# A sum of w_o weights computed two quarter products earlier, and two row turnings one step earlier

## The chip, the cores and the metric

The kernel runs on one core of one Trainium2 chip. A core has five engines with queues of their own: TensorE (PE) multiplies matrices, VectorE (DVE) and ScalarE (ACT) do elementwise work and read the results of PE out of PSUM, GpSimd (POOL) does a little elementwise work and issues some transfers, and SyncE (SP) issues most transfers. Each engine takes its instructions strictly in the order in which they stand in its queue, and engines wait for each other by semaphores.

The metric is the device time of one execution in microseconds, as a median over runs. The kernel before takes 1021.9 us.

## What is computed

One layer of a decoder trunk: a normed input is projected, three mixers (attention, pooling, a state-space scan) are gated and merged, the merged rows are multiplied by `w_o` and added to the input, and the result is normed again and goes through a gated feed-forward block. Everything is float32, with 512 rows (`SEQ`) of 1024 features (`D_MODEL`). The part around the change is this:

```python
merged = gates[:, :, 0] * y_a + gates[:, :, 1] * y_b + gates[:, :, 2] * y_c
x = x + merged @ w_o[i]
x = x + conv_ffn(rmsnorm(x, ln2_g[i]), ffn_w_up[i], ffn_conv_w[i], ffn_conv_b[i], ffn_w_down[i])

def rmsnorm(x, g):
    y = xf * lax.rsqrt(jnp.mean(xf * xf, axis=-1, keepdims=True) + NORM_EPS)
    return (y * g.astype(jnp.float32)).astype(x.dtype)
```

So the rows of `merged @ w_o` are added to `x`, each row is normed over its 1024 features, and the normed rows are the input of the product with `ffn_w_up`.

## The kernel before

Every float32 operand of a matmul is held as two parts of a shorter type: a high part, and a low part that is the operand minus its high part. A product is three passes, high by high, high by low and low by high (`mm3`, L230). For a tile of weights `cast` (L185) writes the high part with two copies on ACT (L195) and `lows` (L210) writes the low part with one subtraction on DVE (L217, tile `wl`).

The program is a list of jobs, and a job is one product with one tile of weights. The loop at L1834 runs over them. Ahead of job n it prepares others (`prepare`, L1841): the low parts of job n+1 on DVE, the casts of job n+2 on ACT, and the load of job n+3. Where `once` is set the casts go out at once; where it isn't they are spread over the next steps (`flush`, L138). Where a job has a `form`, its weights are first computed by it; with `lazy` that is put off to the first spread cast. A job with `late` runs its own preparation inside its body. `step` (L155) advances side work: a generator put into `running` goes on by one `yield` at each step.

PE, ACT, DVE and POOL keep the order in which this program emits their instructions. SP's order is chosen by a scheduler at build time. A pool of tiles hands a buffer out again once its last reader is done: the pool of raw weights (`wraw`, L94) has two buffers and the pool of `W` tiles (`ypool`, L99) has three, so a load waits on SP for the reader that frees its buffer, and what stands behind it on SP waits too.

`merged @ w_o` is `wo_group` (L1265). It is cut into 2 x 2 blocks and done in seven quarter products instead of eight, on sums of blocks. Each multiplies two blocks of 128 rows by 512 features into 512 columns, in 2 x 12 matmuls. In order of execution they are `two`, `five`, `three`, `one`, `six`, `seven`, `four`. The first three share a pair of PSUM banks B, the last four the pair A, on which they pile up: `one` starts the pair, `six`, `seven` and `four` add to it. After each half product DVE reads its bank and adds it to a tile of the new rows `X1` (L1351). The next product may not write a bank before that read is over.

The sums of weights are computed on DVE by `total` (L1376). `W[2]` is `W[0] + W[1]` (L1291). `W[1]` is overwritten by `W[2]` minus the quarter of `one` (L1389). The weights of `four`, the last ones, are a loaded quarter plus `W[2]` (L1387); this sum is lazy, so it is emitted while `six` runs, right after the first read of `six`.

The norm goes on between the products. `first` (L1293) is called behind `one` and `seven`: squares of the first half of a row block on ACT (L439, tile `junk`), a small scale on DVE (L463, L1297), and a multiplication by the gain on POOL (L464, tile `xg`). `then` (L1300) is called behind `six` and `four`, with the second half: squares (L439), a square root on ACT (L473, ahead of the first of which ACT loads a table of functions), reciprocal and scale on DVE (L478 to L483), and the two normed halves, one on DVE (L487) and one on ACT (L488), both tiles named `u`. `norm_turn` (L449) then turns the block: eight transposes on PE into two PSUM banks of the tag `sm` (L453, tile `uT`), two copies on ACT (L456, `uh`), two subtractions on DVE (L457, `ul`). There are four row blocks, tb 0 to 3. For tb 0 and 1 the turning sits in a generator put into `running` with `rest(3)`; for tb 2 and 3 it is called by hand from `opening` (L1522), the first product with `ffn_w_up` (L1533, tile `pu`), which needs the turned rows of tb 0 and 1 and then the low parts of its own weights.

A side item of the same stage is `ff_cols` (L1403): three small loads on SP (L512), two transposes on PE (L518) into two more `sm` banks and two copies on DVE (L519). The tag `sm` has four banks (L101).

## Time and profile before

| | |
|---|---|
| median of 3 runs | 1021.9 us (1021.67 to 1021.9) |
| the profiled execution's own time | 1021.8 us |
| its span, first to last instruction | 1020.0 us |
| PE busy | 1006.3 us (99%) |
| DVE busy | 719.4 us (71%) |
| ACT busy | 518.3 us (51%) |
| POOL busy | 143.8 us (14%) |

All rows come from one profiled execution, and times in them are microseconds from the start of its span. A row of the timeline gives the start, the duration, the engine, the line of the kernel, the operation, the tiles (written <- read), the shapes and how many instructions are merged in it; in square brackets stands how long the engine had been idle before, and what ended that. Instructions of one engine overlap a little, so what an instruction costs its engine is read from its start to the start of the next one. A row of waits gives who waited for whom, the sum in microseconds, how often, and the longest. A row of windows gives the busy time of each engine in a stretch and, under PEclk, the granted clock of TensorE as a share of its full speed.

### The profile page before, as it was taken

What the parts mean: (1) busy time and instruction counts of PE and PEld (TensorE: products, weight loads), DVE (VectorE), ACT (ScalarE), POOL (GpSimd) and SP (SyncE); (2) the same over time, 40 slices, a digit from 0 to 9 for tenths busy, and PEclk for the clock granted to TensorE, in tenths of its full rate; (3) what the DMA queues carried; (4) which work ended last, traced back from release to release, by engine and by line L of the source; (5) the groups of instructions that cost most, each with busy time, mean ns of one, the idle gap of its engine ahead of it and who ended that gap; (6) DMA issues with size and microseconds to landing.
All of it is one profiled execution on the core that took longest, in us unless ns stands there. A gap on an engine that the chain in (4) does not pass through costs nothing.

```text
span 1020.0 us, 13623 instructions
## 1 busy us (share of the span) xinstructions
PE 1006.3 (99%) x5378; PEld 857.5 (84%) x5378; DVE 719.4 (71%) x910; ACT 518.3 (51%) x877; POOL 143.8 (14%) x128
## 2 busy tenths in 40 slices
PE   9999999999999999999999999899999999999997
PEld 8998878999988888888888887698888888888885
DVE  6564768677757647667888787758778768685756
ACT  5433546564435476879566335554444444433434
POOL 1791000010000000000063501102111100111002
PEclk9999999999999999999999999999999999999999
DMA  8548312155254343552256346332332322321332
GB/s 271 168 104 206 101 66 77 56 155 162 95 182 108 90 126 103 145 143 84 83 161 160 124 145 163 129 125 83 105 103 83 105 101 84 124 83 42 124 103 83
DMA packets 114623, 121.26 MB, mean 119 GB/s; under 512 B 6499, under 2 KB 96166, under 8 KB 114559
## 3 DMA queue, kind: packets, MB, share of 16 engines
q1 hardware_dynamic: 111087, 114.81, 36.7%
q0 software_dynamic: 2880, 4.72, 2.8%
q8 instruction: 42, 0.69, 0.3%
q10 hardware_dynamic: 592, 0.86, 0.2%
q14 instruction: 22, 0.18, 0.1%
HBM read 116.58 MB, written 3.00 MB: 117 GB/s over the span
## 4 chain that ended last, share of the span: by engine, by line
PE 95%; DVE 3%; ACT 1%; DMA 1%; issue 0%; ACTq 0%; DVEq 0%
PE pa L238 36%; PE pu L238 22%; PE pb L238 9%; PE pd L238 7%; PE pqk L238 6%; PE pq L238 3%; PE pa L1750 2%; PE ps L786 1%; PE ppw L238 1%; PE po L834 1%; DVE wl L217 1%; PE pt L820 1%; PE py L1119 1%; PE pu L1533 1%; DMA xin<-in_x_dram 1%; ACT junk L439 1%
## 5 line engine op out<-in xcount | busy, mean ns | idle before, releaser
L217 DVE TENSOR_TENSOR wl<-raw,wh 128x2048 fp32r<-128x2048 f32 (+3 forms) x87 | 203.5, 2339 | 47.8 <-ACT wh L195 34.1
L195 ACT CAST wh<-raw 128x1024 fp32r<-128x1024 f32 (+4 forms) x171 | 171.7, 1020 | 68.4 <-DVE raw L361 17.8
L1428 DVE SCALAR_TENSOR_TENSOR hc<-pu,fcol,hc 128x510 f32<-128x510 f32 x88 | 65.8, 748 | 56.4 <-ACT hc L1425 54.8
L238 PE MATMUL pa<-uh,wh 128*128 128x512 f32 (+1 forms) x368 | 88.8, 381 | 0.0
L238 PE MATMUL pa<-ul,wh 128*128 128x512 f32 (+1 forms) x368 | 86.8, 375 | 0.0
L238 PE MATMUL pa<-uh,wl 128*128 128x512 f32 (+1 forms) x368 | 86.7, 375 | 0.0
L238 PE MATMUL pu<-uh,wh 128*128 128x512 f32 (+1 forms) x352 | 83.6, 379 | 0.0
L238 PE MATMUL pu<-ul,wh 128*128 128x512 f32 (+1 forms) x352 | 83.5, 379 | 0.0
L238 PE MATMUL pu<-uh,wl 128*128 128x512 f32 (+1 forms) x352 | 83.5, 379 | 0.0
L238 PEld LDWEIGHTS pa<-ul,wh 128*128 128x128 f32 x368 | 66.7, 188 | 12.6
L238 PEld LDWEIGHTS pa<-uh,wl 128*128 128x128 f32 x368 | 66.7, 188 | 12.5
L238 PEld LDWEIGHTS pa<-uh,wh 128*128 128x128 f32 x368 | 65.4, 189 | 11.8
L238 PEld LDWEIGHTS pu<-ul,wh 128*128 128x128 f32 x352 | 64.2, 188 | 12.5
L238 PEld LDWEIGHTS pu<-uh,wl 128*128 128x128 f32 x352 | 64.2, 188 | 12.4
L238 PEld LDWEIGHTS pu<-uh,wh 128*128 128x128 f32 x352 | 64.1, 188 | 12.4
L1425 ACT ACTIVATE hc<-pu,fcol,fcol 128x512 f32<-128x512 f32 x40 | 31.2, 779 | 79.1 <-PE pu L238 79.1
L1433 POOL TENSOR_TENSOR hc<-hc 128x512 f32<-128x512 f32 x22 | 30.8, 1399 | 286.4 <-DVE hc L1428 252.1
L217 DVE TENSOR_TENSOR wl<-w,wh 128x2048 fp32r<-128x2048 f32 (+1 forms) x22 | 47.3, 2149 | 10.2 <-issue 4.6
L808 ACT ACTIVATE sb<-sb,nmls 128x128 f32<-128x128 f32 (+1 forms) x72 | 30.0, 418 | 31.5 <-DVE nmls L805 20.8
L195 ACT CAST wh<-w 128x1024 fp32r<-128x1024 f32 (+1 forms) x44 | 41.0, 971 | 4.8 <-PE pb L238 2.4
L1102 POOL TENSOR_TENSOR st<-st,dts 128x512 f32<-128x512 f32 x4 | 4.2, 1049 | 226.1 <-ACT st L1110 164.0
L1430 ACT ACTIVATE hc<-hc 128x512 f32<-128x512 f32 x22 | 13.9, 632 | 39.9 <-DVE hc L1428 39.8
(424 smaller groups left out, 1948.4 us busy)
## 6 DMA issues: line engine op xcount, KB each, us to landing
raw<-in_w_in_dram SPq DMA_DIRECT2D x24, 1024.0 KB, 5.5
raw<-in_ffn_w_up_dram SPq DMA_DIRECT2D x22, 1024.0 KB, 5.3
raw<-in_ffn_w_down_dram SPq DMA_DIRECT2D x8, 1024.0 KB
raw<-in_w_in_dram SPq DMA_DIRECT2D x14, 512.0 KB, 5.8
raw<-in_w_in_dram SPq DMA_DIRECT2D x8, 768.0 KB
raw<-in_w_b_dram SPq DMA_DIRECT2D x4, 1024.0 KB
al<-ad SPq DMA_DIRECT2D x16, 256.0 KB, 6.5
raw<-in_w_c_dram SPq DMA_DIRECT2D x4, 1024.0 KB, 5.4
```

The source lines that it names most:

```text
L195: (other.tensor_copy if other and i else act.copy)(job.high[:, :, o], job.raw[:, :, o])
L217: (eng or dve).tensor_tensor(l[:, :, o], job.raw[:, :, o], h[:, :, o].bitcast(F32), OP.subtract)
L238: pe.matmul(ps, l, r, start=first and n == 0, stop=last and n == total - 1, skip_group_check=onto)
L439: act.activation(junk, src, AF.Square, accum_out=ss)
L786: pe.matmul(pss[i][:, o:o + w * P], q[r, n * P:(n + 1) * P], k[r, kb * P:(kb + w) * P], start=True, stop=True)
L808: act.activation(sb[:, off:off + w * P], sb[:, off:off + w * P], AF.Exp, bias=nm[:, n, h:h + 1], accum_out=ls[:, n, h:h + 1])
L820: pe.transpose(pt[:, o:o + P], sb[:, o:o + P], eye)
L1425: act.activation(t, ps, AF.Identity, bias=ff["c1"][:, ff["b"] + m:ff["b"] + m + 1], scale=fw(2, m))
L1428: dve.scalar_tensor_tensor(t[:, sh:], ps[:, :S - sh], fw(k, m), t[:, sh:], OP.mult, OP.add)
L1430: act.activation(t, t, AF.Silu)
L1433: pool.tensor_tensor(a, a, t, OP.mult)
L1750: pe.matmul(first[2 * n + j][:, lo:hi], a[:, k, j * P:(j + 1) * P], b[:, k, lo:hi], start=a is wh and b is uh and k == 0, stop=a is wl and ...
```

## The change

```diff
             if tb < 2:
-                running.append(rest(3))
+                running.append(rest(2))
             elif tb == 2:
...
+        def one_read(tb):
+            first(tb, 1)
+            if tb == 0:
+                total(four.raw, four.raw, W[2])
+
         two = job("A12", quarter(1, 0), None, B, (0, 0), apart=True, fresh=True)
         five = job(1, None, lambda: W[0], B, (1, 1), apart=True, fresh=True)
         three = job(4, None, lambda: W[1], B, (0, 1), more=True)
-        one = job("A11", quarter(0, 0), None, A, (0, 0), behind=lambda tb, h: first(tb, 1))
+        one = job("A11", quarter(0, 0), None, A, (0, 0), behind=lambda tb, h: one_read(tb))
         six = job(2, None, lambda: W[2], A, (0, 1), more=True, op=OP.subtract, behind=then)
         seven = job(3, None, lambda: W[1], A, (1, 1), more=True, op=OP.subtract,
                     behind=lambda tb, h: first(tb, 0))
-        four = job("A22", quarter(1, 0), lambda: total(four.raw, four.raw, W[2]), A, (1, 0), more=True,
+        four = job("A22", quarter(1, 0), None, A, (1, 0), more=True,
                    behind=then)
         one.then = lambda: total(W[1], W[2], one.raw, OP.subtract)
-        six.once, four.lazy = False, True
+        def early():
+            four.load = None
+            fetch(four)
+            four.load = lambda: None
+
+        six.load = early
         four.late, inner = True, four.body
```

The sum for `four` is now emitted behind the first read of `one`, instead of behind the first read of `six`. The load of its quarter is emitted with the preparation of `five`, where `six` used to load nothing, instead of with that of `one`. `four` has no `form` and isn't lazy any more, and `six.once` stays true, so the two casts of `four` go out together at the head of `six`, instead of one in each half of it. The turnings of tb 0 and tb 1 run one step earlier.

In the order of instructions as built this moves the following, and nothing else. On DVE the sum (L1377) stands ahead of the second read of `one`, and the subtractions of tb 0's turning (L457) ahead of the second read of `seven`, those of tb 1's ahead of the first read of `four`. On ACT the two casts stand ahead of the squares of the first half of `six`, and the copies of the turnings (L456) move up likewise. On PE the transposes of tb 0 stand between the two halves of `seven`, right behind those of `ff_cols`, and the transposes of tb 1 between `seven` and `four`; before, they stood between `seven` and `four` and between the halves of `four`. In both kernels tb 1's transposes take the two `sm` banks of `ff_cols` and wait for the copies L519; in the changed one `four` stands behind them in PE's queue. On SP the load of the quarter of `four` keeps its place; one load of `ffn_w_down` (L1481 before, L1491 after) moves ahead of the three loads of `ff_cols`.

## The prediction

> **What bounds the kernel now.** I read the chain of waits first, then the waits of the stage that the change touches (600 to 690 us), then its timelines of PE and DVE.

> ```profile
> PE 95%; DVE 3%; ACT 1%; DMA 1%; issue 0%; ACTq 0%; DVEq 0%
> ```

> PE sets the end, so an edit counts by the PE time that it opens or closes.

> ```profile
> PE pb L238 <- DVE x L1351: 3.0, 2, 1.5
> ```

> Two of PE's waits in this stage are for reads of its banks, and the timeline shows a third of the same length, for the turned rows: 4.5 us together, which is all that can be won.

> ```profile
> 640.64 1.07 PE L238 MATMUL pb<-wh,sah 128*128 128x512 f32 x4
> ...
> 643.37 1.07 PE L238 MATMUL pb<-wh,sbh 128*128 128x512 f32 x4
> ...
> 646.09 0.27 PE L518 MATMUL fcol0p<-eye,fcol0r 128*128 128x128 f32 x1
> ...
> 648.04 1.21 PE L238 MATMUL pb<-wh,sbh 128*128 128x512 f32 x4 [1.49 <-DVE x L1351]
> ...
> 650.94 1.03 PE L453 MATMUL uT<-eye,u 128*128 128x128 f32 x8
> 653.45 1.17 PE L238 MATMUL pb<-wh,mgh 128*128 128x512 f32 x4 [1.47 <-DVE x L1351]
> ...
> 656.30 1.03 PE L453 MATMUL uT<-eye,u 128*128 128x128 f32 x8
> 657.09 1.17 PE L238 MATMUL pb<-wh,mgh 128*128 128x512 f32 x4
> ...
> 661.56 2.18 PE L1533 MATMUL pu<-uh,wh 128*128 128x256 f32 x16 [1.49 <-ACT uh L456]
> ...
> 665.50 1.03 PE L453 MATMUL uT<-eye,u 128*128 128x128 f32 x8
> 666.63 2.18 PE L1533 MATMUL pu<-uh,wl 128*128 128x256 f32 x16
> ```

> The halves of `seven` start at 643.37 and 648.04, those of `four` at 653.45 and 657.09, the opening of the next product at 661.56. Each half ends in a read on DVE, and the reads stand in DVE's queue among everything else:

> ```profile
> 637.15 0.15 DVE L1297 TENSOR_SCALAR vo<-v 128x1 f32<-128x1 f32 x1
> 638.12 0.69 DVE L1351 TENSOR_TENSOR x<-x,pb 128x512 f32<-128x512 f32 x1 [0.82 <-PE pb L238]
> ...
> 639.86 2.47 DVE L217 TENSOR_TENSOR wl<-w,wh 128x2048 fp32r<-128x2048 f32 x1
> 642.25 0.68 DVE L1351 TENSOR_TENSOR x<-x,pb 128x512 f32<-128x512 f32 x1
> ...
> 643.80 2.29 DVE L1377 TENSOR_TENSOR raw<-raw,w 128x2048 f32<-128x2048 f32 x1
> 646.00 0.16 DVE L481 RECIPROCAL r<-sq 128x1 f32<-128x1 f32 x1
> ...
> 646.64 0.75 DVE L487 SCALAR_TENSOR_TENSOR u<-x,rt,grow 128x512 f32<-128x512 f32 x1
> 647.31 0.68 DVE L1351 TENSOR_TENSOR x<-x,pb 128x512 f32<-128x512 f32 x1
> ...
> 652.63 0.68 DVE L1351 TENSOR_TENSOR x<-x,pb 128x512 f32<-128x512 f32 x1
> ...
> 654.36 0.28 DVE L519 COPY fcol<-fcol0p 128x128 f32<-128x128 f32 x1
> ...
> 654.67 0.68 DVE L1351 TENSOR_TENSOR x<-x,pb 128x512 f32<-128x512 f32 x1
> ...
> 656.61 1.29 DVE L457 TENSOR_TENSOR ul<-uT,uh 128x512 fp32r<-128x512 f32 x2
> 657.81 0.68 DVE L1351 TENSOR_TENSOR x<-x,pb 128x512 f32<-128x512 f32 x1
> ...
> 661.54 1.29 DVE L457 TENSOR_TENSOR ul<-uT,uh 128x512 fp32r<-128x512 f32 x2 [0.53 <-ACT uh L456]
> 662.74 0.68 DVE L1351 TENSOR_TENSOR x<-x,pb 128x512 f32<-128x512 f32 x1
> ...
> 664.29 2.28 DVE L217 TENSOR_TENSOR wl<-raw,wh 128x2048 fp32r<-128x2048 f32 x1
> ```

> The reads pace PE: at 643.80 the moved sum stands between two reads, 2.20 us from its start to that of the next. The last row matters most: PE's start at 666.63 is the end of that subtraction plus 0.06. So the stage is a chain through DVE and ACT, and the question is when the instruction of 664.29 starts.

> **The sum, step by step along DVE.** The sum can start right behind the scale, at 637.15 + 0.07 = 637.22; PE makes DVE wait there 0.82 today. Its cost is 2.20 at least. It may be 2.39: the subtraction at 639.86 took 2.47 where the same-sized sum took 2.29, and POOL was busy during its start:

> ```profile
> 636.26 1.29 POOL L464 TENSOR_TENSOR xg<-x,grow 128x512 f32<-128x512 f32 x1 [6.98 <-DVE x L1351]
> 638.89 1.29 POOL L464 TENSOR_TENSOR xg<-x,grow 128x512 f32<-128x512 f32 x1 [1.34 <-DVE x L1351]
> ```

> The sum would start 0.33 before POOL's earlier row ends, as the subtraction did before the later one, so I lean to 2.39 and keep both. The second read of `one` then starts at 639.42 to 639.61 instead of 638.12: 1.30 to 1.49 late. It ends by 640.3, and the half of `six` that needs its bank starts at 640.64: no stall, by 0.3. The first read of `six` follows 4.13 behind, as before (638.12 to 642.25): 643.55 to 643.74.

> There the old gain is due: without the sum, the way to the next read should shrink by 2.20. It doesn't, since the reciprocal needs the square root, and that a table:

> ```profile
> 643.70 1.28 ACT L473 ACT_TABLE_LOAD   x1
> 645.00 0.30 ACT L473 ACTIVATE sq<-ss,v 128x1 f32<-128x1 f32 x1
> 646.17 1.04 ACT L195 CAST wh<-raw 128x1024 fp32r<-128x1024 f32 x1 [0.88 <-DVE r L481]
> ```

> The load starts 1.45 behind the read and the root is done 3.05 behind it. With 0.03 for the semaphore the reciprocal can start 3.08 behind, where today it starts 3.75 behind (642.25 to 646.00). Of 2.20 only 0.67 comes back; the sum had covered the load. The next read follows the reciprocal by 1.31: 647.94 to 648.13, 0.63 to 0.82 late. The two casts of `four`, 1.04 each (the last row is one of them), now stand ahead of this on ACT, between the squares of the second read of `one` (done near 641) and the first read of `six` at 643.55: they fit. [...]

> Low parts of `four` and the first read of `seven`: 5.32 on, unchanged, 653.26 to 653.45. The copy of `ff_cols` 1.73 behind that: 654.99 to 655.18. Then the subtractions of tb 0's turning, 1.20 for the pair (656.61 to 657.81), ahead of the second read of `seven`: 2.04 + 1.20 behind the first, 656.50 to 656.69. On to the first read of `four` the queue holds tb 1's pair where it held tb 0's: 3.14 as before, 659.64 to 659.83. From there the pair of 661.54 and the 0.53 waited ahead of it are gone: 4.93 - 1.73 = 3.20, or 3.11 with the overlap of neighbours, so the last read starts at 662.75 to 663.03 instead of 662.74. Everything behind it is as before. **Net: 0.0 to 0.3 us, taken as 0.2.** Saved are the two waits of 0.82 and 0.53, and they are paid for by the table load.

> **The same on PE**, to see that it isn't later. The first half of `seven` waits for the read of `six` (0.73 from its start): 644.3 to 644.5, 0.9 to 1.1 late. It ends 2.72 later, at 647.0 to 647.2, the small transposes take until 647.7, and tb 0's `u` is written 1.39 behind the reciprocal, 648.0 to 648.2. Its eight transposes take 0.79 (656.30 to 657.09). The second half of `seven`, 2.90 long, starts at 648.8 to 649.0 and ends at 651.7 to 651.9. Now tb 1's transposes stand ahead of `four` and wait for the copy of 654.99: 655.3 to 655.5. **PE stands still for about 3.6 us in one piece**, where it stood 1.47. Then 0.79, 2.85 and 2.73: `four` begins at 656.1 to 656.3, and the opening at 661.7 to 661.9 (before, 661.56). The first half of `four` ends 0.5 before DVE reads it. The opening's first two passes take 3.94 and the transposes 0.79, so PE is ready at 666.4 to 666.6 for a subtraction that is done at 666.64 to 666.93. PE has 0.2 to 0.3 to spare.

> **Loads.**

> ```profile
> 611.60 0.38 SPq L182 DMA_DIRECT2D raw<-in_w_o_dram  x1
> ...
> 632.01 0.54 SPq L512 DMA_DIRECT2D fcol0r<-in_ffn_conv_w_dram  x1
> ...
> 642.39 4.11 SPq L1481 DMA_DIRECT2D w<-in_ffn_w_down_dram  x2
> ```

> The quarter of `four` is issued at 611.60, once its buffer is free, and that stays: the moved load is worth nothing either way. The first of the two `ffn_w_down` loads goes out when the sum frees `W[2]`, at 639.5 instead of 642.39, and the three loads of `ff_cols` now wait behind it, from 632.0 to about 640. PE needs them at 647; a delay up to about 652 falls into the standstill of 3.6.

> **Rivals.** *PE's clock falls in the long standstill* (slower).

> ```profile
> 645.00:650.00 5.00, 3.51 (x16) 2.59 (x15) 3.83 (x11) 3.91 (x8) 0.00 (x0) 1.00 0.86 316
> ...
> 1013.40:1017.00 3.60, 0.00 (x0) 0.00 (x0) 2.57 (x7) 1.74 (x4) 0.00 (x0) 1.00 0.38 146
> 1017.00:1020.00 3.00, 0.00 (x0) 0.00 (x0) 0.00 (x0) 0.00 (x0) 0.00 (x0) 0.50 0.45 175
> ```

> Behind the last matmul the clock stays at 1.00 for 3.6 us and is then 0.50; a stop of 1.5, which lies in the first of these stretches, left it at 1.00. It decides from a stop of about 3.6 on, which is what I work out. If half speed lasts as long as it took to come, 3.6 us, PE loses 1.8, less the 0.2 to spare: 1021.8 + 0.2 + 1.6 = 1023.6. If it lasts over the transposes and both halves of `four`, 6.4 us are lost: 1028.2. Against it: a stop just short of the limit costs nothing. [...]

> *The table load starts earlier or is hidden* (faster): then the reciprocal waits its 1.28 less, 1022.0 - 1.3 = 1020.7. Against it: the load stands behind the squares in ACT's order. *All three stops close*: 1021.8 - 4.45 = 1017.4. Against it: DVE's chain above; it needs PE to bound the stage.

> *The loads of `ff_cols` are late* (slower). They were issued at 632.01 and used at 646.09, so they take 14.1 at most. From 640.5 that is 654.6; with the small transposes, tb 0's and the second half of `seven` (0.5 + 0.79 + 2.90) tb 1's would start at 658.8, 3.3 late, less the 0.5 by which `four` is early for its read: 1022.0 + 2.8 = 1024.8. For it: a whole 1 MB load now stands ahead of them. Against it: they need be no faster than 11.

> **How the numbers follow.** The profiled execution took 1021.8, 0.1 under the median of 1021.9. Forecast: 1021.8 + 0.2 = 1022.0, its own range 1021.5 to 1022.4. Chances: forecast 0.58; clock 0.18, of which 0.10 near 1023.6 and 0.08 beyond; table hidden 0.07; stops closed 0.06; late loads 0.06; something unseen 0.05, mostly slower. Two runs of this kernel can be told apart from about 0.2%, 2.0 us: forecast, near clock and hidden table lie within, 0.75; slower 0.08 + 0.06 + 0.03 = 0.17; faster 0.06 + 0.02 = 0.08. The range goes from the hidden table to the first clock case and the late loads, 1020.5 to 1024.8.

> **What would show it.** Right: the sum at 637.2, the read behind it 1.3 to 1.5 late, the reciprocal 3.1 behind the first read of `six`, one stop of PE of 3 to 4 us ahead of tb 1's transposes released by L519, none ahead of the opening, and the start of 666.63 within 0.4 of that. Wrong: a granted clock under 1.00 near 655, a stop of PE at L518 released by a transfer, or two reads of `seven` closer than 3 us.

## The result, and the profile after

| | before | after |
|---|---|---|
| median | 1022.04 us (1021.64 to 1022.77, 22 runs) | 1023.58 us (1021.7 to 1027.55, 22 runs) |
| the profiled execution's own time | 1021.8 us | 1024.06 us |
| its span | 1020.0 us | 1022.3 us |
| its mean granted clock | 0.999 | 0.997 |

After over before is 1.0017, 95% interval 1.001 to 1.0024. That is under the 0.2% that the prediction called no change, and inside its range, but it isn't the forecast of 1022.0: it is the time of the first rival, 1023.6.

Of the 2.26 us between the two profiled executions, 0.69 are there before the changed part begins: DVE's small scale ahead of the moved sum stands at 637.15 in the profile before and at 637.84 after. Nearly all of it (0.66) comes from the start of the run, where DVE's first scaling of `xin` stands at 19.59 and 20.25. That start differs between the profiled executions here (19.51 in `banks_free` to 21.24 in `fill`). So all distances below are counted from that scale, L1297, which I call the mark. DVE's timeline after (start, duration, engine, line, operation, tiles, shapes):

```profile
637.84 0.15 DVE L1297 TENSOR_SCALAR vo<-v 128x1 f32<-128x1 f32 x1
637.91 2.47 DVE L1377 TENSOR_TENSOR raw<-raw,w 128x2048 f32<-128x2048 f32 x1
640.31 0.68 DVE L1351 TENSOR_TENSOR x<-x,pb 128x512 f32<-128x512 f32 x1
...
644.43 0.68 DVE L1351 TENSOR_TENSOR x<-x,pb 128x512 f32<-128x512 f32 x1
...
647.50 0.16 DVE L481 RECIPROCAL r<-sq 128x1 f32<-128x1 f32 x1 [1.45 <-ACT sq L473]
...
648.82 0.68 DVE L1351 TENSOR_TENSOR x<-x,pb 128x512 f32<-128x512 f32 x1
...
654.14 0.68 DVE L1351 TENSOR_TENSOR x<-x,pb 128x512 f32<-128x512 f32 x1
...
655.87 0.28 DVE L519 COPY fcol<-fcol0p 128x128 f32<-128x128 f32 x1
...
657.37 0.68 DVE L1351 TENSOR_TENSOR x<-x,pb 128x512 f32<-128x512 f32 x1
...
661.74 0.69 DVE L1351 TENSOR_TENSOR x<-x,pb 128x512 f32<-128x512 f32 x1 [1.14 <-PE pb L238]
...
666.41 2.29 DVE L217 TENSOR_TENSOR wl<-raw,wh 128x2048 fp32r<-128x2048 f32 x1
```

Down to 657.37 every row stands within 0.01 of the upper end of what the prediction worked out for it (less 0.69: 637.22, 639.62, 643.74, 648.13, 653.45, 655.18, 656.68). The wait of 1.45 in front of the reciprocal, 3.07 behind the read of 644.43, is the table load laid bare. ACT's timeline after:

```profile
645.88 1.28 ACT L473 ACT_TABLE_LOAD   x1
647.18 0.29 ACT L473 ACTIVATE sq<-ss,v 128x1 f32<-128x1 f32 x1
```

Then the row of 661.74, the first read of `four`, waits for PE, which was meant to be half a microsecond early. PE's timeline and windows say why (in a window's row, PEclk stands behind the five engines' busy times, ahead of the DMA share):

```profile
651.76 1.07 PE L238 MATMUL pb<-wl,sbh 128*128 128x512 f32 x4
656.29 1.06 PE L453 MATMUL uT<-eye,u 128*128 128x128 f32 x8 [3.46 <-DVE fcol L519]
657.12 1.82 PE L238 MATMUL pb<-wh,mgh 128*128 128x512 f32 x4
658.73 1.91 PE L238 MATMUL pb<-wh,mgl 128*128 128x512 f32 x4
660.44 1.26 PE L238 MATMUL pb<-wl,mgh 128*128 128x512 f32 x4
661.54 1.09 PE L238 MATMUL pb<-wh,mgh 128*128 128x512 f32 x4
...
664.28 2.08 PE L1543 MATMUL pu<-uh,wh 128*128 128x256 f32 x16
666.20 2.08 PE L1543 MATMUL pu<-ul,wh 128*128 128x256 f32 x16
668.12 1.04 PE L453 MATMUL uT<-eye,u 128*128 128x128 f32 x8
668.91 2.15 PE L1543 MATMUL pu<-uh,wl 128*128 128x256 f32 x16
```

```profile
655.00:657.40 2.40, 1.10 (x9) 1.13 (x10) 1.76 (x7) 1.53 (x4) 1.16 (x1) 1.00 0.79 244
657.40:660.80 3.40, 3.40 (x9) 2.67 (x8) 2.25 (x6) 1.69 (x4) 1.28 (x1) 0.50 0.40 136
660.80:665.00 4.20, 4.20 (x23) 3.53 (x21) 2.19 (x7) 1.74 (x4) 0.00 (x0) 1.00 0.00 0
```

The one long stop is there, 3.46 us, released by L519. Behind it four matmuls of `four` take 1.6 to 1.7 us from start to start instead of 0.91, for 3.4 us, in which the granted clock is 0.50. The clock doesn't fall in the stop, but 1.1 us behind its end. The third pass of the opening starts 668.91 - 637.84 = 31.07 behind the mark. Before it was 666.63 - 637.15 = 29.48: 1.59 more. Nothing waits in front of it now: PE goes from the transposes of 668.12 straight on, so PE has become the bound.

### The profile page after: what moved, and what is told of

It is laid out like the page before. It is cut to its first block, busy times and chain, and to the rows that moved or that the text cites. A ratio compares the mean times of both kernels' runs of the same rounds, so it can differ in the third digit from the quotient of the medians.

```text
span 1022.3 us, 13624 instructions
## 1 busy us (share of the span) xinstructions
PE 1007.1 (99%) x5378; PEld 858.1 (84%) x5378; DVE 718.6 (70%) x910; ACT 518.7 (51%) x877; POOL 143.7 (14%) x128
## 4 chain that ended last, share of the span: by engine, by line
PE 96%; DVE 2%; DMA 1%; ACT 1%; issue 0%; ACTq 0%; DVEq 0%
PE pa L238 36%; PE pu L238 22%; PE pb L238 10%; PE pd L238 7%; PE pqk L238 6%; PE pq L238 3%; PE pa L1760 2%; PE ps L786 1%; PE pu L1543 1%; PE ppw L238 1%; PE po L834 1%; PE pt L820 1%; PE py L1119 1%; DVE wl L217 1%; DMA xin<-in_x_dram 1%; PE pyo L1126 1%
## 5 line engine op out<-in xcount | busy, mean ns | idle before, releaser
L217 DVE TENSOR_TENSOR wl<-raw,wh 128x2048 fp32r<-128x2048 f32 (+3 forms) x87 | 202.7, 2330 | 47.6 <-ACT wh L195 33.9
L195 ACT CAST wh<-raw 128x1024 fp32r<-128x1024 f32 (+4 forms) x171 | 171.5, 1020 | 63.4 <-DVE raw L361 17.8
L238 PE MATMUL pa<-uh,wh 128*128 128x512 f32 (+1 forms) x368 | 88.8, 381 | 0.0
L238 PE MATMUL pa<-ul,wh 128*128 128x512 f32 (+1 forms) x368 | 86.8, 375 | 0.0
L238 PE MATMUL pa<-uh,wl 128*128 128x512 f32 (+1 forms) x368 | 86.8, 375 | 0.0
L238 PE MATMUL pu<-uh,wh 128*128 128x512 f32 (+1 forms) x352 | 83.5, 379 | 0.0
L238 PE MATMUL pu<-ul,wh 128*128 128x512 f32 (+1 forms) x352 | 83.5, 379 | 0.0
L238 PE MATMUL pu<-uh,wl 128*128 128x512 f32 (+1 forms) x352 | 83.5, 379 | 0.0
L238 PEld LDWEIGHTS pa<-ul,wh 128*128 128x128 f32 x368 | 66.7, 188 | 12.6
L238 PEld LDWEIGHTS pa<-uh,wl 128*128 128x128 f32 x368 | 66.7, 188 | 12.5
L238 PEld LDWEIGHTS pa<-uh,wh 128*128 128x128 f32 x368 | 65.4, 189 | 11.8
L238 PEld LDWEIGHTS pu<-uh,wl 128*128 128x128 f32 x352 | 64.2, 188 | 12.5
L238 PEld LDWEIGHTS pu<-ul,wh 128*128 128x128 f32 x352 | 64.2, 188 | 12.5
L238 PEld LDWEIGHTS pu<-uh,wh 128*128 128x128 f32 x352 | 64.1, 188 | 12.4
L217 DVE TENSOR_TENSOR wl<-w,wh 128x2048 fp32r<-128x2048 f32 (+1 forms) x22 | 47.3, 2151 | 10.2 <-issue 4.6
L195 ACT CAST wh<-w 128x1024 fp32r<-128x1024 f32 (+1 forms) x44 | 41.0, 971 | 4.8 <-PE pb L238 2.4
```

Source lines behind the costliest of these rows:

```text
L195: (other.tensor_copy if other and i else act.copy)(job.high[:, :, o], job.raw[:, :, o])
L217: (eng or dve).tensor_tensor(l[:, :, o], job.raw[:, :, o], h[:, :, o].bitcast(F32), OP.subtract)
L238: pe.matmul(ps, l, r, start=first and n == 0, stop=last and n == total - 1, skip_group_check=onto)
```

## The experiments

Each kernel ran together with the kernel before on one chip. Two measures are given beside the time: the distance from the mark to the third pass in the profiled execution, and how many of the runs had a mean granted clock of 0.997 or less. In the profiles a clock that falls only behind the last matmul gives 0.998 (`fill`) to 0.999 (before); one stretch of 3.41 us at half speed more gives 0.996 (`turn_only`) to 0.997 (after). Of the kernel before 13 runs of 100 beside these were so too, at 1024.3 to 1025.3, none of them with a profile.

**PE's stop filled.** Twelve matmuls whose result nobody reads, behind tb 0's two reads of `seven`:

```diff
                     read(i)
+                    if j == 3 and i:
+                        for _ in range(12):
+                            pe.matmul(B[0], wh[:, 0, :P], wl[:, 0, :], start=True, stop=True)
```

> Twelve extra matmuls (2.7 us of PE) on finished weights, into a PSUM bank that nobody reads any more, stand behind the second half of seven, inside the long stop of PE; nothing else differs from the changed kernel. Clock theory: the extra 1.5 us of the changed kernel are half-clock stretches that the stop sets off, so with the stop filled the granted clock is 0.999 in every run and the time falls to 1021.8 to 1022.6, with a spread under 1.5 us. Chain theory: the extra time is in DVE's chain (the sum ahead of a read, the table load laid bare), which no matmul touches, so 1023.6 as without them. If both share it, 1022.8.

Median 1022.07 (11 runs), ratio 1.0000, 0.9992 to 1.0009. No run at 0.997 or less. The profiled run is the slowest of the eleven, 1023.51, with its mark 1.51 later than before. Its PE timeline:

```profile
653.49 2.88 PE L1370 MATMUL pb<-wl,wh 128*128 128x512 f32 x12
657.11 1.06 PE L453 MATMUL uT<-eye,u 128*128 128x128 f32 x8 [0.74 <-DVE fcol L519]
657.93 1.17 PE L238 MATMUL pb<-wh,mgh 128*128 128x512 f32 x4
...
668.34 2.17 PE L1546 MATMUL pu<-uh,wl 128*128 128x256 f32 x16
```

The mark is at 638.66 here, so the third pass starts 29.68 behind it, 0.20 later than before. More work on PE makes the kernel 1.5 us faster (1023.58 and 1022.07 in two batches; over the kernel before beside each, 1.0017 and 1.0000): what was lost was the clock, and 0.20 is what DVE's chain alone costs.

**The banks of `ff_cols` out of the way.** Its two transposes come two steps later, so tb 1's transposes needn't wait for L519:

```diff
-            yield
-            yield
+            for _ in range(4):
+                yield
             t0()
```

> The changed kernel with the two small transposes of ff_cols and their copies (L518, L519) two steps later, between the halves of four, so that tb 1's transposes find two free banks and wait for their own rows alone. Clock theory: PE's stop ahead of four is cut in two by the transposes, the longer part near 2 us, the clock stays at 1.00, and the time is 1021.8 to 1022.5. Chain theory: DVE's work and order are the same save for 0.3 us of copies, so 1023.6.

A miss: median 1023.81 (12 runs), ratio 1.0012, 1.0002 to 1.0022, and 8 of 12 runs at 0.997 or less. The long stop was gone, but PE, now earlier, had a new one further on:

```profile
664.10 1.04 PE L453 MATMUL uT<-eye,u 128*128 128x128 f32 x8
667.03 2.79 PE L1543 MATMUL pu<-uh,wl 128*128 128x256 f32 x16 [1.90 <-DVE wl L217]
```

```profile
667.00:668.30 1.30, 1.27 (x10) 1.27 (x11) 1.19 (x4) 0.70 (x2) 0.00 (x0) 1.00 0.10 15
668.30:671.70 3.40, 3.40 (x18) 3.40 (x17) 2.87 (x3) 0.98 (x3) 0.00 (x0) 0.50 0.90 303
```

PE stood still for 1.90 only, and the clock fell 1.3 behind that stop's end. So a stop much shorter than the predicted 3.6 was enough here. DVE's chain sets the end; moving PE's waiting about doesn't remove it.

**One part of the change at a time.** The sum and the load moved, but the turnings with `rest(3)` as before:

```diff
-                running.append(rest(2))
+                running.append(rest(3))
```

> The changed kernel with the turnings of tb 0 and tb 1 back where they were (three steps): the sum, its casts and the load alone are moved. Clock theory: no stop longer than about 2 us, clock 0.999; the reads of six are 0.6 to 0.8 us late and nothing is won back later, so 1022.6 to 1022.9, steady from run to run. Chain theory: the sum is what costs, 1023.6 or more, steady too.

Median 1023.07 (11 runs), ratio 1.0009, 0.9999 to 1.0019; two runs at 0.997 or less. That is a little over the 1022.6 to 1022.9 expected, and not steady: those two took 1025.57 and 1026.28. In the profile the mean granted clock was 0.999, the stops 1.04, 1.03, 1.42 and 1.57, and the third pass started at 668.87 with the mark at 638.58: 30.29, 0.81 later than before. The moved sum alone costs that much on DVE, since the wait of 0.53 ahead of the second pair of L457 stays. And the kernel before with only the turnings one step up, `rest(2)` for `rest(3)`:

> The kernel before with the turnings one step earlier and nothing else: the sum stays under the table load. Clock theory: tb 1's transposes wait for the copies here as well, PE stands still for about 3.1 us, and the clock falls in part of the runs: near 1021.5 where it stays (DVE's chain is 0.5 us shorter), 1022.6 to 1023.2 where it falls, so a spread of over 1 us. Chain theory: 1021.5 in all runs, 0.5 us faster than before, since the sum is not moved.

Median 1022.55 (1021.07 to 1024.09, 11 runs), ratio 1.0002, 0.9993 to 1.0011, in two groups that overlap: three runs with the clock up, 1021.07 to 1022.55, median 1021.52, and eight at 0.996 to 0.997, 1022.1 to 1024.09, median 1022.79. Its profile fell into the second group:

```profile
655.33 1.94 PE L453 MATMUL uT<-eye,u 128*128 128x128 f32 x8 [3.04 <-DVE fcol L519]
656.92 1.89 PE L238 MATMUL pb<-wh,mgh 128*128 128x512 f32 x4
```

So with its stop of 3.04 the turnings bring the fall, and the sum brings DVE's part. A second profile of the same kernel (the label is `turn_fill`, but nothing is filled in it):

> A second look at the kernel before with the two turnings alone one step up, for the place of the fall: theory: if the clock falls, it does so 0 to 3.4 us behind the stop at tb 1's transposes, for 3.41 us; if the record shows full clock throughout, the time is 1022.1 at most.

1023.38, with a stop of 3.04 again, and half clock from 655.57 to 658.98. In the first profile it was 655.08 to 658.49, ahead of the stop's end at 655.33; here 655.57 is ahead of 655.65. Where the fall stands against the stop is not fixed.

**Does any work of PE hold the clock?** In the fall of the changed kernel PE's eight transposes lay between the stop and the first product. The filler again, with 30 transposes `pe.transpose(B[0][:, :P], X1[0, 0][:, :P], eye)` in place of the twelve matmuls:

> The changed kernel with 30 more transposes of 128x128 on PE, results unused, behind tb 0's two reads of `seven`, so that they fill the stop ahead of tb 1's transposes (30 at about 0.1 us is 3.0 of 3.46). Theory A (the clock follows any work of PE): as with the twelve matmuls, mean clocks of .998 to .999 in every run and a median of 1021.9 to 1022.4. Theory B (transposes don't hold the clock, only products do; PE is without a product for 4.3 us all the same): most runs at .997 or below, one stretch of 3.41 us at half clock behind the start of `four` in the profile, median 1023.3 to 1023.9.

Median 1022.74 (11 runs), ratio 1.0005, 0.9996 to 1.0014; the kernel before had 1022.55 beside it. Nine of 11 runs kept the clock. PE had no product between 652.78, where the last one ended, and 657.07, and the clock was 1.00 throughout (windows 652.60 to 658.00):

```profile
652.63 3.44 PE L1370 MATMUL pb<-eye,x 128*128 128x128 f32 x30
656.25 1.06 PE L453 MATMUL uT<-eye,u 128*128 128x128 f32 x8 [0.18 <-DVE fcol L519]
657.07 1.17 PE L238 MATMUL pb<-wh,mgh 128*128 128x512 f32 x4
...
667.48 2.17 PE L1546 MATMUL pu<-uh,wl 128*128 128x256 f32 x16
```

Theory A held, for a clock that was already full; whether transposes also bring it up was not tested. From the mark at 637.79 the third pass is 29.69 away, the 0.20 of `fill` once more.

**How long a stop is too long?** Six and eight of the unused matmuls instead of twelve:

> The changed kernel with six instead of twelve of the unused matmuls ahead of tb 1's transposes, so that the stop left is about 3.46 - 6 x 0.23 = 2.1. Theory A (the clock is set by fixed stretches of 3.41 whose phase against the kernel differs from run to run, and one in which PE stood for over half, 1.71, is followed by a stretch at half clock): the stop falls so that neither side of a stretch's border reaches 1.71 in (2 x 1.71 - 2.1) / 3.41 = 38% of the runs; about 6 or 7 of 11 runs at .997 or below and near 1023.5, the others near 1022.1. Theory B (PE must stand for a whole stretch, or for about 3 us on end): no run falls but for the one in ten of the kernel before, median 1021.9 to 1022.3.

> The same with eight of them, so that the stop left is about 1.65. Theory A (over half of a stretch, 1.71): no stretch can have that much of it, so no run falls but for the one in ten that also falls in the kernel before; mean clocks .998 to .999, median 1021.9 to 1022.3. If the limit is lower than half a stretch (say 1.2 to 1.5), several of 11 runs are at .997 or below.

With six: median 1022.96 (12 runs), ratio 1.0002, 0.9993 to 1.001, four of 12 at 0.997 or less. The profiled run, 1023.32, is one of these, with a fall behind a stop of 2.10, and a third pass 668.16 - 637.12 = 31.04 behind the mark:

```profile
655.57 1.06 PE L453 MATMUL uT<-eye,u 128*128 128x128 f32 x8 [2.10 <-DVE fcol L519]
656.39 1.84 PE L238 MATMUL pb<-wh,mgh 128*128 128x512 f32 x4
658.03 1.91 PE L238 MATMUL pb<-wh,mgl 128*128 128x512 f32 x4
```

With eight: median 1022.88 (11 runs), ratio 0.9997, 0.9988 to 1.0007, one of 11; the kernel before had 1022.61 in this batch. Its stop was 1.65, and the third pass 667.60 - 637.92 = 29.68 behind the mark. The fall of the profiled run with six speaks against theory B. But theory A had reckoned with 6 or 7 of 12 such runs, and found four, three of which (1024.5 to 1024.8) can be what the kernel before shows as well, six times in 23 in this batch. The share was wrong; that a stop of 2.1 can do it is shown by one profile.

**The table of functions loaded early.** One square root of a constant, behind the first squares of `one`:

```diff
             nxt[tb] = v0, vh, xg
+            if (tb, h) == (0, 1):
+                act.activation(small("early", [P, 1]), eps, AF.Sqrt)
```

> The changed kernel with one square root more on ACT, of a constant, behind the first squares of `one`, so that the table of functions is loaded before the first read of `six`. Theory (the table load sets the step from the first read of `six` to the next read): the reciprocal comes 1.7 to 1.9 us behind that read instead of 3.07, everything behind it on DVE 1.2 earlier, PE's stop ahead of tb 1's transposes 2.2 to 2.5 instead of 3.46. With the transposes PE is then without a product for 3.0 to 3.3 us, under the 3.41 of one stretch of the clock's record: few runs fall, median 1020.7 to 1021.3. If the stop still drops the clock in most runs: 1022.2 to 1022.8. Rival (the load is not on the path, something else ends last): the reads stand where they stood, 1023.3 to 1023.9.

Median 1022.92 (11 runs), ratio 1.0002, 0.9993 to 1.001: 0.1 over what was expected for the case that the stop still drops the clock in most runs, and it did so in nine of 11. The step on DVE did what was expected, the reciprocal came 1.79 behind the read of `six`:

```profile
644.50 0.68 DVE L1353 TENSOR_TENSOR x<-x,pb 128x512 f32<-128x512 f32 x1
...
646.29 0.16 DVE L481 RECIPROCAL r<-sq 128x1 f32<-128x1 f32 x1 [0.17 <-ACT sq L473]
```

The stop shrank to 2.71 (2.2 to 2.5 were expected) and still dropped the clock. So the gain on DVE was there and the clock took it. With six of the unused matmuls in the stop beside it:

> The same as with the early square root, with six of the unused matmuls of `fill` in the stop ahead of tb 1's transposes (1.3 us of 2.2). Theory: no fall of the clock in any run and no time lost to the six: 1020.7 to 1021.1, faster than before by 1.1 to 1.5. If the median is more than 0.4 under that without the six, the clock still fell there. Rival (the gain of the early table is eaten by PE, which becomes the bound behind `four`): 1021.6 to 1022.1.

> The same kernel as `early_table_fill` once more, since its interval ended close to 1. If the third pass of the opening starts 1.07 earlier after DVE's scale than in the kernel before, as it did in that profile, the ratio is 0.9985 to 0.9995 and the clock stays up in all runs but the one in seven of the kernel before. Rival (that batch was lucky): a ratio of 0.9995 to 1.0005.

1021.72 (11 runs), ratio 0.999, 0.9981 to 0.9999, and once more 1020.69 (11 runs), 0.9988, 0.9979 to 0.9997. One of 22 runs fell. The third pass starts 665.82 - 637.41 = 28.41 behind the mark in the first profile, 1.07 earlier than before. The first time is over what was expected of it, 1020.7 to 1021.1, and falls into the rival's 1021.6 to 1022.1, but in a batch in which the kernel before took 1022.55; the earlier third pass speaks against the rival, in which PE eats the gain, and the second time meets the expectation. PE's timeline and ACT's of the first:

```profile
651.72 1.52 PE L1372 MATMUL pb<-wl,wh 128*128 128x512 f32 x6
654.59 1.07 PE L453 MATMUL uT<-eye,u 128*128 128x128 f32 x8 [1.35 <-DVE fcol L519]
655.41 1.17 PE L238 MATMUL pb<-wh,mgh 128*128 128x512 f32 x4
```

```profile
637.21 1.28 ACT L1300 ACT_TABLE_LOAD   x1
638.50 0.20 ACT L1300 ACTIVATE early<-eps 128x1 f32<-128x1 f32 x1
640.59 0.63 ACT L439 ACTIVATE junk<-x 128x512 f32<-128x512 f32 x1 [1.89 <-DVE x L1353]
```

ACT has 1.89 to spare behind the load there, and the change with these two additions beats both kernels: 0.8 and 1.2 us under the one before beside it, and 1.9 and 2.9 under the median of the changed one, which ran in another batch.

## Why the prediction was right, and where it was wrong

*The sum along DVE: right.* The sum took 2.47, which puts 2.40 between its start and the next read's: the leaned-to end of 2.20 to 2.39, and POOL's row (636.95 to 638.24) stands beside its start at 637.91 as in the rows quoted. That POOL's work is what made it longer was not tested. The second read of `one` came 1.50 late, the reciprocal 3.07 behind the read of `six`, the first read of `seven` 5.32 behind the second of `six`, and the second of `seven` 3.23 on. The net of 0.2 was never seen in the changed kernel's own profile; the three kernels in which only the clock was held up show it, 0.20, 0.21 and 0.20 (`fill`, `transposes`, `fill_8`).

*The table load as the price: right.* Where it is taken off the path, the third pass comes 1.07 earlier than before, which is 1.27 less than 0.20: the load's 1.28, as the rival "hidden" had it.

*The loads: right.* `ff_cols` went out at 640.91 to 641.79 instead of 632.01, and PE used them at 648.10 with no wait for them.

*PE's timetable: right up to the stop.* It was 3.46 for "about 3.6", in one piece, and `four` began 0.1 later than the span given. The spare of 0.2 to 0.3 is right too: in `transposes` the third pass waits 0.22 for L217.

*The clock: wrong, and this decided the time.* The step that failed is "It decides from a stop of about 3.6 on, which is what I work out", with "a stop just short of the limit costs nothing". The 3.6 was read from one row, the fall behind the last matmul. That delay is not a constant: it was 2.21 to 4.61 us. The clock's entries in the traces against the end of the last matmul:

| kernel | last matmul ends | clock falls | delay |
|---|---|---|---|
| before | 1013.37 | 1016.99 | 3.62 |
| after | 1015.62 | 1019.21 | 3.59 |
| `fill` | 1015.07 | 1017.46 | 2.39 |
| `early_table` | 1014.20 | 1016.41 | 2.21 |
| `early_table_fill` | 1012.55 | 1016.70 | 4.15 |
| `banks_free` | 1015.25 | 1019.86 | 4.61 |

How long PE stood in the 3.41 us that end with the fall: after 653.98 to 656.29, 2.31; `turn_only` 2.79; `early_table` 2.23; `fill_6` 2.10; `banks_free` 1.90. Stops of 1.49 (before) and 1.57 (`sum_only`) lay whole in one stretch and left the clock up. The stop of 1.65 in `fill_8` says less: it was cut by a border, at 655.21, with 1.17 behind it. The rows of `sum_only` and `fill_8`:

```profile
663.80 2.18 PE L1543 MATMUL pu<-uh,wh 128*128 128x256 f32 x16 [1.57 <-ACT uh L456]
```

```profile
656.38 1.06 PE L453 MATMUL uT<-eye,u 128*128 128x128 f32 x8 [1.65 <-DVE fcol L519]
```

So in these profiles the limit lies between 1.57 and 1.90 in one stretch of 3.41, near its half. Then a stop of 3.46 nearly always puts more than that into one stretch, wherever the border falls, and 19 of 22 runs fell:

| kernel | longest stop, us | runs at 0.997 or less | median of the others | of these |
|---|---|---|---|---|
| after | 3.46 | 19 of 22 | 1022.31 | 1023.63 |
| `turn_only` | 3.04 | 8 of 11 | 1021.52 | 1022.79 |
| `early_table` | 2.71 | 9 of 11 | 1021.83 | 1022.93 |
| `fill_6` | 2.10 | 4 of 12 | 1022.70 | 1024.53 |
| `banks_free` | 1.90 | 8 of 12 | 1022.33 | 1023.90 |
| `fill_8` | 1.65 | 1 of 11 | 1022.84 | 1024.68 |
| `sum_only` | 1.57 | 2 of 11 | 1023.03 | 1025.92 |
| before, beside these | 1.49 | 13 of 100 | 1022.27 | 1024.62 |
| `early_table_fill`, twice | 1.36 | 1 of 22 | 1021.00 | 1023.74 |
| `fill` | 1.04 | none of 11 | 1022.07 | |
| `transposes` | 1.04 | 2 of 11 | 1022.69 | 1025.07 |

The rival's price was near: 1.6 net, and 31.07 - 29.68 = 1.39 in the profile. That is luck in part: it took half speed to last as long as its coming, 3.6, which elsewhere is 2.21 or 4.61; half speed lasted 3.41. Its chance of 0.18 should have been that of the forecast. By the prediction's own signs, too, a granted clock under 1.00 near 655 spoke against it, and the start that was at 666.63 is 1.59 later, not within 0.4. Only the wide range, drawn to take in the rivals, holds the result; the forecast's own, 1021.5 to 1022.4, doesn't.

Left open: that the border's place against the kernel decides in each run was inferred from the profiles and shares and not set by hand; the exact limit; why `fill_6` fell in only four of 12 runs, less than `banks_free` and than the half that even a limit of 1.90 gives it, (2 x 1.90 - 2.10) / 3.41 being 0.50; where the rare falls of the kernel before come from, which cost about 2.4 us; and the changed kernel's five runs at 0.994 or 0.995 (1024.58 to 1027.55), which by that clock lost more than one stretch, and of which none has a profile.

## What to carry to other kernels

In these profiles a stop of the matrix engine cost more than its own length where 1.9 us or more of it lay in one clock stretch of 3.41: 3.46 us in one piece lost 1.4 us more behind it, while the three stops of 1.5 before, at a granted clock of 1.00 from 645 to 665, lost nothing beyond their own length. So when a change gathers small waits into one, price the clock too, and don't read a limit from a single row whose phase is free: ask other executions. The stop could be bridged with unused work, twelve matmuls (none of 11 runs at 0.997 or less) or 30 transposes (two of 11), but first look for what makes it long: here a 1.28 us table load that the moved sum had covered.

## What was not expected of the hardware

- The clock fell 1.1 to 1.3 us behind the end of a stop, with PE at work, after stops of 3.46 (after), 2.10 (`fill_6`) and 1.90 (`banks_free`).
- Behind the last matmul it fell after 2.21 to 4.61 us, though the kernels end alike.
- Transposes of 128 x 128 kept the clock at 1.00 for 4.3 us without a product (652.78 to 657.07 in `transposes`).
- The start of the run, up to the first scaling of `xin`, differs by up to 1.73 us between profiled executions (19.51 to 21.24), so two profiles are compared by distances from a common mark.
